# One SBUF pool moves behind three others: u's high and low parts go from 16K to 104K of a partition

## The chip, the cores and the metric

The kernel runs on one core of a Trainium2 chip. The metric is device time in microseconds: 467.73 us, the median of three runs (467.04 to 467.74).

## What is computed

One residual block of a decoder with 512 tokens and 1024 channels, all in float32. `u = rms_norm(x)` is multiplied by one wide input matrix (5912 columns). Its columns become the queries, keys, values and gates of two attention branches of 8 heads each (A: compressed, selected and sliding-window attention; B: block-sparse attention), the SiLU gates z of both, and two merge gates:

```python
u = rms_norm(x, norm_pre)
proj = u @ w_in
y_a = nsa_attention(...) * silu(z_a);  y_b = moba_attention(...) * silu(z_b)
m = sigmoid(gate_a) * (y_a @ w_a) + sigmoid(gate_b) * (y_b @ w_b)
out = x + rms_norm(m @ w_o, norm_post)
```

At 512 tokens all blocks that could be selected are selected, so the attention of both branches is causal over whole 512-token rows.

## The kernel before

**Two parts for each operand.** Every float32 operand of a large product is split into a high part and a low part (the rest), and a product is three matmuls: high by high, high by low, low by high. `u` lies transposed in two tiles `uh` and `ul`, 128 partitions by 8 slices of 512 tokens (16 KB of a partition each). In `mm(out, held, streamed)` the second argument is the operand held in the array, which a weight load (PEld in the profile) brings in before each matmul; the third is streamed through it.

**The work.** The input columns come in chunks of 256: 20 chunks (kcvc, ksw, qa0, qa1, za0, za1, zb0, zb1, qkb0 to 3, ga0 to 3, gb0 to 3) go through `proj`, two halves of 24 matmuls each, which hold a 128x128 piece of the split weights (`ws`, pool `wspl`) and stream 512 tokens of `uh` or `ul` (L171 to L173). That makes 20 x 48 = 960 matmuls that stream u. The two chunks vb0 and vb1 do it the other way round: they hold a piece of `uh` or `ul` and stream 256 columns of `ws` (L294 to L296), 192 matmuls. Four chunks ab0 to ab3 use the same `proj` for `y @ w_a` and `y @ w_b`: they hold `ws` and stream `ys`, y's two parts (192 matmuls of 512 columns). wo0 holds `m`, the merged result, and streams `ws` (L416 to L418, 96 matmuls); wo1 holds `m` and streams `wo1h` (L1118 to L1120).

```python
171            mm(dst, v[:, 0, k], rh(n), start=(n == 0), stop=False)        # rh: uh or ys
172            mm(dst, v[:, 0, k], rl(n), start=False, stop=False)           # rl: ul or ys
173            mm(dst, v[:, 1, k], rh(n), start=False, stop=(n == len(kts) - 1))
294            mm(o, uh[:, kk, a], v[:, 0, k], start=first, stop=False, skip_group_check=True)
416            mm(o, mst[kk][:, 0, a], v[:, 0, k], start=(kk == 0), stop=False)
417            mm(o, mst[kk][:, 0, a], v[:, 1, k], start=False, stop=False)
418            mm(o, mst[kk][:, 1, a], v[:, 0, k], start=False, stop=(kk == KT - 1))
1118           mm(o, mst[k][:, 0, a], wo1h[:, 0, k, w], start=(k == 0), stop=False)
1119           mm(o, mst[k][:, 0, a], wo1h[:, 1, k, w], start=False, stop=False)
1120           mm(o, mst[k][:, 1, a], wo1h[:, 0, k, w], start=False, stop=(k == KT - 1))
```

**The order.** TensorE's order is written out by hand. First the norm and transposes of x and a small projection (to 25.6 us), then kcvc and ksw in one row (96 matmuls), w1 and qa, then the attention of 24 units, 80 to 327 us. Each unit has scores (L953 streams the high part of k, L954 its low part `klos`, both hold q), transposes of the probabilities p (L992), and the product with v (L1008, L1009 stream the transposed p, `pt`, and hold v); between these stand pieces of the projection chunks, most of them three steps of `proj`, so 9 matmuls in a row. Along the timeline the 960 matmuls that stream u stand in 3 rows of 96 (kcvc with ksw, ga2 with gb2, ga3 with gb3), 2 of 24, 5 of 18, 52 of 9, 9 of 6 and 4 of 3. After the attention come ab0, ab1, ga2, gb2, ab2, ga3, gb3, ab3, wo0 and wo1 with the last norm.

**Where the tiles lie.** A pool takes the next free bytes of each partition when it is opened, and each small tile is rounded up to 32 bytes. The first pool begins at byte 16,512 (16K and 128 bytes). The pools in their order, with the byte addresses that follow:

| pool | what it holds | from byte (K) | offset in 512 bytes of its tiles |
|---|---|---|---|
| const, 52,192 bytes | uh, ul, ident, klos, vcs, small ones | 16,512 (16.1K); ul 32,896 | uh, ul 128; klos 160; vcs 96 |
| wraw, 2 x 8 KB | raw weights | 68,704 (67.1K) | 96 |
| wspl, 3 x 8 KB | `ws`, split weights | 85,088 (83.1K) | 96 |
| s4, 12 x 4 KB | shared homes: q, k, v, ys, kcsl, gates, m_4, m_5 | 109,664 (107.1K) | 96 |
| zp, 4 x 4 KB | z, later m_0 to m_3 | 158,816 (155.1K) | 96 |
| small | statistics | 175,200 (171.1K) | |
| early, att, mp in turn | x; pt, p, bias; wo1h, m_6, m_7 | 179,744 (175.5K) | pt, wo1h, m_6, m_7: 32 |

All slices that a matmul takes of these tiles begin at multiples of 512 bytes from there, so the last column holds for them too (a slice of q, k, v, u, ws, ys, m or wo1h).

Of the kernel before, what the change touches and what calls it, by code (L numbers as in the profile page):

```python
# [41 lines left out]
def hybrid_block(ctx, tc, x, norm_pre, w_in, pe_k, w1_k, w2_k, pe_v, w1_v, w2_v,  # L42
# [10 lines left out]
    def enter(**kw):  # L53
        return ctx.enter_context(tc.tile_pool(**kw))

    const = enter(name="const", bufs=1)
    wraw = enter(name="wraw", bufs=2)
    wspl = enter(name="wspl", bufs=3)
    psum = enter(name="psum", bufs=2, space=PSUM)
    s4 = enter(name="s4", bufs=12)  # L60
    zp = enter(name="zp", bufs=4)
    small = enter(name="small", bufs=2)

# [1101 lines left out]
```

## Time and profile before

| | |
|---|---|
| median of 3 runs | 467.73 us |
| profiled execution | 467.33 us, its span 465.6 us |
| granted TensorE clock, mean | 0.997 |
| TensorE busy | 457.3 us (98%) of 2408 matmuls |
| VectorE, ScalarE, GpSimd busy | 322.8, 253.6, 123.4 us |
| moved from and to HBM | 41.6 MB, 89 GB/s over the span |

TensorE's matmuls overlap: one takes some 390 ns from its start to its modelled end, and the next starts before that. What a matmul costs in a full row is therefore read as the distance between two starts, and best over a row of many: (last start - first start) / number of steps. The start times of the timeline have 10 ns, so a row of 20 steps gives 0.5 ns.

### The profile page before, as it was taken

How to read it: one execution, taken by the hardware profiler on the slowest of the kernel's cores; microseconds unless marked ns; L12 is line 12 of the kernel's file. 1: busy time of each engine (PE TensorE's matmuls, PEld its weight loads, DVE VectorE, ACT ScalarE, POOL GpSimd, SP SyncE). 2: the span in 40 equal slices, each digit the busy share in tenths (PEclk: the TensorE clock that was granted, in tenths of full speed). 3: DMA queues.
4: the chain of work that ended last, by engine and by line, in shares of the span. 5: the costliest groups of instructions: out<-in, count | busy, mean ns of one | idle time of the engine just before them, and what ended most of it. 6: DMA issues, size and time to landing. Idle time of an engine off the chain costs nothing.

```text
span 465.6 us, 7014 instructions
## 1 busy us (share of the span) xinstructions
PE 457.3 (98%) x2408; PEld 389.7 (84%) x2408; DVE 322.8 (69%) x830; ACT 253.6 (54%) x684; POOL 123.4 (26%) x143
## 2 busy tenths in 40 slices
PE   8999999999999999999999999999999999999994
PEld 6988887889999888888888888888888888888884
DVE  3868768898878768778897878786674263275044
ACT  5845556666666566566766756675433333234021
POOL 2540008312432313423154454332221020020000
PEclk9999999999999999999999999999999999999998
DMA  8666225023302204032131221132235323223133
GB/s 275 196 181 182 62 49 162 13 80 92 78 15 92 74 18 109 8 88 92 23 114 48 66 92 49 44 92 90 61 103 145 100 52 129 90 90 137 45 137 135
DMA packets 45731, 43.13 MB, mean 93 GB/s; under 512 B 1752, under 2 KB 39936, under 8 KB 45696
## 3 DMA queue, kind: packets, MB, share of 16 engines
q1 hardware_dynamic: 45552, 42.17, 30.9%
q10 hardware_dynamic: 144, 0.52, 0.4%
q8 instruction: 19, 0.31, 0.3%
q14 instruction: 16, 0.13, 0.1%
HBM read 39.54 MB, written 2.10 MB: 89 GB/s over the span
## 4 chain that ended last, share of the span: by engine, by line
PE 97%; DMA 1%; DVE 0%; ACT 0%; SPq 0%; POOLq 0%; issue 0%; POOL 0%; DVEq 0%; ACTq 0%
PE t L992 6%; PE o L1009 3%; PE o L1008 3%; PE s L953 3%; PE mm_ga L171 3%; PE mm_ga L172 3%; PE mm_gb L171 3%; PE mm_gb L172 3%; PE mm_gb L173 3%; PE mm_ga L173 3%; PE mm_qkb L171 3%; PE mm_qkb L172 3%; PE mm_qkb L173 3%; PE s L954 3%; PE pa L640 3%; PE mm_qa L171 2%
## 5 line engine op out<-in xcount | busy, mean ns | idle before, releaser
L959 ACT ACTIVATE p<-p,st 128x512 f32<-128x512 f32 (+3 forms) x96 | 53.2, 555 | 42.0 <-DVE st L957 41.8
L971 POOL TENSOR_SCALAR p<-p,st 128x256 f32<-128x256 f32 (+1 forms) x48 | 43.8, 922 | 68.3 <-DVE st L968 51.5
L994 DVE TENSOR_TENSOR pt<-t,pt 128x512 fp32r<-128x512 f32 (+1 forms) x72 | 39.1, 591 | 3.6 <-ACT pt L993 3.4
L993 ACT ACTIVATE pt<-t 128x512 fp32r<-128x512 f32 (+1 forms) x72 | 32.8, 528 | 9.5 <-PE t L992 9.0
L957 DVE CUSTOM_DVE_ANT_0 p<-s,bias_a 128x512 f32<-128x512 f32 (+3 forms) x64 | 29.1, 485 | 11.4 <-PE s L954 11.1
L358 POOL TENSOR_TENSOR ga<-ga,gb 128x512 f32<-128x512 f32 x8 | 11.7, 1464 | 76.3 <-DVE gb L357 76.3
L992 PE MATMUL t<-ident,p 128*128 128x128 f32 x240 | 30.1, 273 | 0.0
L992 PEld LDWEIGHTS t<-ident,p 128*128 128x128 f32 x240 | 27.1, 141 | 0.8
L1020 POOL TENSOR_TENSOR z<-ot,z 64x512 f32<-64x512 f32 x16 | 20.7, 1293 | 24.3 <-DVE ot L1019 24.3
L119 DVE TENSOR_TENSOR ws_ab<-raw_ab,ws_ab 128x256 fp32r<-128x256 f32 x32 | 12.7, 454 | 20.0 <-ACT ws_ab L118 20.0
L971 DVE TENSOR_SCALAR p<-p,st 128x512 f32<-128x512 f32 (+1 forms) x48 | 25.6, 570 | 0.6
L171 PE MATMUL mm_qkb<-uh,ws_qkb 128*128 128x512 f32 x64 | 25.8, 404 | 0.0
L171 PE MATMUL mm_ga<-uh,ws_ga 128*128 128x512 f32 x64 | 25.6, 400 | 0.0
L171 PE MATMUL mm_gb<-uh,ws_gb 128*128 128x512 f32 x64 | 25.6, 400 | 0.0
L173 PE MATMUL mm_gb<-uh,ws_gb 128*128 128x512 f32 x64 | 25.3, 395 | 0.0
L173 PE MATMUL mm_ga<-uh,ws_ga 128*128 128x512 f32 x64 | 25.3, 395 | 0.0
L172 PE MATMUL mm_ga<-ul,ws_ga 128*128 128x512 f32 x64 | 25.3, 395 | 0.0
L172 PE MATMUL mm_gb<-ul,ws_gb 128*128 128x512 f32 x64 | 25.2, 394 | 0.0
L173 PE MATMUL mm_qkb<-uh,ws_qkb 128*128 128x512 f32 x64 | 25.2, 394 | 0.0
L172 PE MATMUL mm_qkb<-ul,ws_qkb 128*128 128x512 f32 x64 | 25.2, 394 | 0.0
L911 POOL TENSOR_SCALAR bias_b<-dbase 128x512 f32<-128x512 f32 x8 | 12.3, 1535 | 36.7 <-DVE st L957 36.7
L911 POOL TENSOR_SCALAR bias_a<-dbase 128x512 f32<-128x512 f32 x8 | 13.0, 1620 | 33.2 <-DVE st L957 33.0
(309 smaller groups left out, 1379.5 us busy)
## 6 DMA issues: line engine op xcount, KB each, us to landing
raw_qkb<-in_w_in_dram SPq DMA_DIRECT2D x8, 512.0 KB, 5.2
raw_ga<-in_w_in_dram SPq DMA_DIRECT2D x4, 1024.0 KB, 5.5
raw_gb<-in_w_in_dram SPq DMA_DIRECT2D x4, 1024.0 KB, 5.2
raw_wo<-in_w_o_dram SPq DMA_DIRECT2D x4, 1024.0 KB, 5.0
raw_qa<-in_w_in_dram SPq DMA_DIRECT2D x4, 512.0 KB, 6.6
raw_za<-in_w_in_dram SPq DMA_DIRECT2D x4, 512.0 KB, 5.2
raw_vb<-in_w_in_dram SPq DMA_DIRECT2D x2, 1024.0 KB, 5.2
raw_zb<-in_w_in_dram SPq DMA_DIRECT2D x2, 1024.0 KB, 5.7
```

Of the source, the lines that this page charges most:

```text
L171: mm(dst, v[:, 0, k], rh(n), start=(n == 0), stop=False)
L172: mm(dst, v[:, 0, k], rl(n), start=False, stop=False)
L173: mm(dst, v[:, 1, k], rh(n), start=False, stop=(n == len(kts) - 1))
L640: mm(pt[:, 0:280], u[:, k, a], wa_hl[:, h, k], start=(n == 0 and k == 0), stop=(n == last and k == KT - 1))
L911: pool.tensor_scalar(t, dbase, slope, None, op0=ALU.mult)
L957: dve.tensor_tensor_reduce(pp, src, bias[:, 384 - 128 * i:512], 1.0, 3.0e38, ALU.add, ALU.min, st[:, 0, i:i + 1])
L959: act.activation(pp, pp, AF.Exp, bias=st[:, 0, i:i + 1], scale=-1.0, accum_out=st[:, 1, i:i + 1])
L971: (dve if i >= 2 else pool).tensor_scalar(pp, pp, st[:, 1, i:i + 1], None, op0=ALU.mult)
L992: pe_eng.transpose(tp[:, b * 128:(b + 1) * 128], p_of(u, i)[:, 128 * j:128 * j + 128], ident)
L993: act.activation(h[:, c0:c0 + n], tp[:, 0:n], AF.Copy)
L994: dve.tensor_tensor(l[:, c0:c0 + n], tp[:, 0:n], f(h[:, c0:c0 + n]), op=ALU.subtract)
L1020: pool.tensor_tensor(zs[zt][mine], t[mine], zs[zt][mine], op=ALU.mult)
```

## The change

`const` is opened after `s4` instead of first. Nothing else differs.

```diff
-    const = enter(name="const", bufs=1)
     wraw = enter(name="wraw", bufs=2)
     wspl = enter(name="wspl", bufs=3)
     psum = enter(name="psum", bufs=2, space=PSUM)
     s4 = enter(name="s4", bufs=12)
+    const = enter(name="const", bufs=1)
     zp = enter(name="zp", bufs=4)
     small = enter(name="small", bufs=2)
```

By the sizes of the table wraw, wspl and s4 move down by 52,192 bytes (wraw to 16.1K, wspl to 32.1K, s4 to 56.1K), and const moves up by 90,112 bytes (uh to 104.1K, ul to 120.1K, klos to 136.6K). From zp on all stays. psum is another memory.

## Rows read from the trace of the kernel before

**Rows 1.** The page's first part, TensorE: busy time, share of the span, instructions.
```profile
PE 457.3 (98%) x2408; PEld 389.7 (84%) x2408; DVE 322.8 (69%) x830; ACT 253.6 (54%) x684; POOL 123.4 (26%) x143
```

**Rows 2.** The waits of TensorE over the whole span: all that it waited for, us in total, times, longest.
```profile
PE warmup L664 <- DVE warmup L83: 1.4, 1, 1.4
PE ut L592 <- DVE diag L579: 0.7, 1, 0.7
```

**Rows 3.** TensorE's instructions grouped by line and shape: busy us, mean ns of one from its start to its modelled end, idle before. Second part of the product, in a gate chunk (streams ul) and in the two halves of the ab chunks (stream ys).
```profile
L172 PE MATMUL mm_ga<-ul,ws_ga 128*128 128x512 f32 x64 | 25.3, 395 | 0.0
...
L172 PE MATMUL pa<-ys_a,ws_ab 128*128 128x512 f32 x32 | 12.4, 389 | 0.0
...
L172 PE MATMUL pb<-ys_b,ws_ab 128*128 128x512 f32 x32 | 12.4, 389 | 0.0
```

**Rows 4.** Timeline of TensorE in gb3 (streams u): start us, us, engine, line, tiles. The first and the last row shown are 20 steps apart.
```profile
399.33 0.40 PE L171 MATMUL mm_gb<-uh,ws_gb 128*128 128x512 f32 x1
...
404.00 0.40 PE L173 MATMUL mm_gb<-uh,ws_gb 128*128 128x512 f32 x1
```

**Rows 5.** The same timeline, going on: the first eight matmuls of ab3 (streams ys), and two later ones that are 24 steps apart.
```profile
404.23 0.40 PE L171 MATMUL pa<-ys_a,ws_ab 128*128 128x512 f32 x1
404.48 0.39 PE L172 MATMUL pa<-ys_a,ws_ab 128*128 128x512 f32 x1
404.70 0.39 PE L173 MATMUL pa<-ys_a,ws_ab 128*128 128x512 f32 x1
404.93 0.40 PE L171 MATMUL pa<-ys_a,ws_ab 128*128 128x512 f32 x1
405.17 0.39 PE L172 MATMUL pa<-ys_a,ws_ab 128*128 128x512 f32 x1
405.39 0.40 PE L173 MATMUL pa<-ys_a,ws_ab 128*128 128x512 f32 x1
405.63 0.39 PE L171 MATMUL pa<-ys_a,ws_ab 128*128 128x512 f32 x1
405.86 0.39 PE L172 MATMUL pa<-ys_a,ws_ab 128*128 128x512 f32 x1
...
407.22 0.39 PE L172 MATMUL pb<-ys_b,ws_ab 128*128 128x512 f32 x1
...
412.66 0.39 PE L172 MATMUL pb<-ys_b,ws_ab 128*128 128x512 f32 x1
```

**Rows 6.** Timeline of wo0 (holds m, streams ws): its first matmul, and 72 steps later the first one that holds m_6. The 24 steps from there, with m_6 and m_7, end at the first row of group 7.
```profile
415.15 0.39 PE L416 MATMUL wo<-ws_wo,m 128*128 128x512 f32 x1
...
431.47 0.39 PE L416 MATMUL wo<-ws_wo,m 128*128 128x512 f32 x1
```

**Rows 7.** Timeline of wo1 (holds m, streams wo1h): the first matmul, with m_0; 18 steps later the first of the six that hold m_6 and m_7; and the one after these six, with m_0 again.
```profile
436.96 0.39 PE L1118 MATMUL wo<-wo1h,m 128*128 128x512 f32 x1
...
441.16 0.40 PE L1118 MATMUL wo<-wo1h,m 128*128 128x512 f32 x1
441.40 0.39 PE L1119 MATMUL wo<-wo1h,m 128*128 128x512 f32 x1
441.62 0.39 PE L1120 MATMUL wo<-wo1h,m 128*128 128x512 f32 x1
441.86 0.40 PE L1118 MATMUL wo<-wo1h,m 128*128 128x512 f32 x1
442.09 0.39 PE L1119 MATMUL wo<-wo1h,m 128*128 128x512 f32 x1
442.32 0.39 PE L1120 MATMUL wo<-wo1h,m 128*128 128x512 f32 x1
442.55 0.40 PE L1118 MATMUL wo<-wo1h,m 128*128 128x512 f32 x1
```

**Rows 8.** Busy time in three stretches: us, then busy us and instructions of PE, PEld, DVE, ACT, POOL, then granted TensorE clock, DMA share, GB/s. The first streams u, the second is wo1, the third wo0.
```profile
364.00:366.00 2.00, 2.00 (x10) 1.60 (x9) 0.00 (x0) 0.49 (x1) 0.00 (x0) 1.00 0.00 0
...
439.00:441.00 2.00, 2.00 (x10) 1.58 (x10) 0.00 (x0) 0.00 (x0) 0.00 (x0) 1.00 0.00 0
...
415.00:417.00 2.00, 2.00 (x11) 1.65 (x10) 1.65 (x3) 1.15 (x2) 0.88 (x1) 1.00 1.05 408
```

**Rows 9.** Timeline of one row of 9 that stream u, in the attention: the second matmul, and the first score 8 steps later. There are 52 such rows.
```profile
97.66 0.39 PE L172 MATMUL mm_za<-ul,ws_za 128*128 128x512 f32 x1
...
99.52 0.39 PE L953 MATMUL s<-k_ks,q_a 128*128 128x512 f32 x1
```

**Rows 10.** Timeline of matmuls of 256 columns: vb0, two rows 11 steps apart; then wo1's second cut, two rows 5 steps apart with m_4 and m_5 held, and two rows 5 steps apart with m_6 and m_7 held.
```profile
129.01 0.28 PE L294 MATMUL mm_vb<-ws_vb,uh 128*128 128x256 f32 x1
...
130.31 0.28 PE L296 MATMUL mm_vb<-ws_vb,ul 128*128 128x256 f32 x1
...
455.10 0.28 PE L1118 MATMUL wo<-wo1h,m 128*128 128x256 f32 x1
...
455.67 0.28 PE L1120 MATMUL wo<-wo1h,m 128*128 128x256 f32 x1
455.78 0.28 PE L1118 MATMUL wo<-wo1h,m 128*128 128x256 f32 x1
...
456.38 0.28 PE L1120 MATMUL wo<-wo1h,m 128*128 128x256 f32 x1
```

## The prediction

> **What bounds the kernel.** I read the page's first part and TensorE's waits first: TensorE is busy 98% of the span [rows 1], and it waited 2.1 us in all, both times within the start-up [rows 2]. After that no other engine and no DMA holds it up; the time is the sum of the distances between the starts of its matmuls. The change moves only addresses: it adds, removes and reorders no instruction, DMA or wait. So it can act only if a matmul's own pace depends on where its operands lie. I went to the groups by shape to see whether it does, and it does: the same 128x512 matmul on the same line has a mean of 395 ns when it streams ul and 389 ns when it streams ys [rows 3]. The timeline says what that is per step. In gb3, 20 steps take 404.00 - 399.33 = 4.67 us, 233.5 ns each [rows 4]. In ab3, once it runs evenly, 24 steps take 412.66 - 407.22 = 5.44 us, 226.7 ns each [rows 5]; wo0's first 72 take 431.47 - 415.15 = 16.32 us, again 226.7 [rows 6]; wo1's first 18 take 441.16 - 436.96 = 4.20 us, 233.3 [rows 7]. There are two paces, 233.3 and 226.7 ns, 6.6 ns apart.
>
> The clock is not the reason: it is granted in full, the 2.4 GHz level, in stretches of all three kinds. Nor is other traffic: wo1 goes at 233.3 in a stretch where VectorE, ScalarE, GpSimd and DMA do nothing at all, u's stretch is nearly as quiet, and wo0 goes at 226.7 with the DMA engines at a share of 1.05 and three engines busy [rows 8]. The addresses are left. Two accounts fit the even stretches.
>
> *Offset.* What counts is the distance between the streamed operand and the held one, whose next piece is loaded while the present one streams, within 512 bytes (the last column of the table of pools). ab streams 96 and holds 96: distance 0, 226.7. wo0 with m_0 to m_5: 96 and 96, 0, 226.7. u's matmuls: 128 - 96 = 32, 233.5. wo1 with m_0 to m_5: 32 - 96 = -64, 233.3. wo0 with m_6 and m_7: 96 - 32 = 64, and its 24 steps take 436.96 - 431.47 = 5.49 us, 228.8 ns [rows 6, 7].
>
> *Place.* Every pair at 226.7 lies with both operands between 83K and 172K of the partition; u (16K to 48K) and wo1h (179K to 212K) lie outside.
>
> One stretch separates them. In wo1 the six steps with m_6 and m_7 have distance 0 (32 and 32), but both operands lie above 179K. They should be slow by place. By offset they should do what ab3 does when it comes in from another distance, and it takes ab3 seven steps to run evenly: the lengths are 0.40, 0.39, 0.39, 0.40, 0.39, 0.40 [rows 5]. The six steps of wo1 show 0.40, 0.39, 0.39, 0.40, 0.39, 0.39, and their starts stand alike, the first step long (0.25 and 0.24 us), the second short (0.22 in both), then 0.22 to 0.24; that is 1.39 us / 6 = 231.7 ns on average, under the 233.3 before them [rows 5, 7]. They enter the even pace as ab3 does; six steps are too few to reach it. That is why I take the offset account.
>
> **The change part by part, by offset.** const moves up by 90,112 bytes, 176 x 512, so uh, ul, klos and vcs keep their offsets. wraw, wspl and s4 move down by 52,192 bytes, 101 x 512 + 480, so their offset goes from 96 to 128. zp and what lies behind it stay.
>
> 1. *u streams, ws held: 32 becomes 0.* 960 matmuls. In a row of 96 the first steps are the entry. ab3's entry of seven steps takes 405.86 - 404.23 = 1.63 us, 232.9 ns each [rows 5], so the entry gains nothing over 233.3, and each step after it gains 6.6 ns. In the rows of 9 the pace now is (99.52 - 97.66) / 8 = 232.5 ns [rows 9], so a step there gains 5.8. How long the entry is after a score, a transpose or a product with v, no row shows for distance 0. Seven steps is the long end, from ab3; the short end is one. I take four, as the entries here do not come out of the 233.3 pattern that ab3 came from. Rows of 96: 3 x 91 x 6.6 = 1.80 us. Rows of 24: 2 x 19 x 6.6 = 0.25. Of 18: 5 x 13 x 5.8 = 0.38. Of 9: 52 x 4 x 5.8 = 1.21. Of 6: 9 x 1 x 5.8 = 0.05. Sum -3.7 us; with entries of seven steps -2.5, with one step -5.0.
> 2. *vb: ws streams, u held, -32 becomes 0.* 192 matmuls of 256 columns. Now (130.31 - 129.01) / 11 = 118.2 ns. At distance 0 the only row of this shape is wo1 with m_6 and m_7: (456.38 - 455.78) / 5 = 120 ns; the fastest that this shape shows anywhere is (455.67 - 455.10) / 5 = 114 ns [rows 10]. I take 120, the row with the same distance: 192 x 1.8 = +0.35 us; the other end is 192 x -4.2 = -0.8.
> 3. *wo0 with m_0 to m_3 (zp): 0 becomes 32.* 48 matmuls go from 226.7 to 233.3: +0.32 us. With m_4 and m_5 both operands move alike: 0. With m_6 and m_7 64 becomes 96, which no row shows: between 226.7 and 233.3 from 228.8 now, -0.05 to +0.1 us.
> 4. *ab, and the high part of k against q:* both operands lie in wspl or s4 and move alike: 0.
> 5. *The rest of the attention.* klos against q goes from 64 to 32, pt against v from -64 to -96, wo1 with m_4 and m_5 likewise, w1's two chunks shift too. These are some 300 matmuls, and no row shows -96. With the two paces as ends each could gain or lose up to 3 ns on average: -0.9 to +0.9 us. I take 0.
> 6. *The other engines* run the same instructions on tiles that lie elsewhere. TensorE waits for none of them [rows 2], so it costs nothing, as long as they keep their lead; with TensorE 0.7% faster and VectorE at 69% [rows 1] I put nothing on a wait that comes out.
>
> Sum: -3.7 + 0.35 + 0.32 = -3.0 us. The profiled execution took 467.33 us (span 465.6), 0.4 under the median of the runs, so the sum gives 464.3 for it and 464.7 for a median; I say 464.5. The ends: -5.0 - 0.8 + 0.3 - 0.9 = -6.4, and -2.5 + 0.35 + 0.4 + 0.9 = -0.9; all terms will not fall on one side, so this case's own range is 462.0 to 466.4.
>
> **A rule against it.** The rows show two steady paces for one form of instruction with the clock at full [rows 4, 5, 8]. The Trainium skill, "TensorE: Matmul & The Clock Gate", in its Part 2 ("Step-by-step"), says that the array reads the streamed and the held operand through two independent ports, so that loading the next weights takes nothing from the running matmul; under "Back-to-back issue gap" it gives 215.7 ns for 512 columns as its figure. By that, addresses play no part and the change is worth 0: 467.3 to 467.7. The trace does not agree with it, at 226.7 and 233.3.
>
> **Rivals.**
> - *Place of both operands (slower).* The even pace needs both operands between 83K and 172K, and one outside costs the full 6.6 ns. u is then inside, but ws, at 32K to 56K, is out: u's matmuls stay at 233.3. ab holds ws and loses 192 x 6.6 = 1.27 us, wo0 streams it and loses 72 x 6.6 = 0.48 with m_0 to m_5 and 24 x 4.5 = 0.11 with m_6 and m_7. That is +1.9 us, 469.4. It decides if a held operand alone at 32K is enough to slow a stream from 104K. For it: all even stretches lie inside. Against it: the six steps of wo1 [rows 7], and m_6 held at 211K cost wo0 2.1 ns a step, not 6.6 [rows 6]. Chance 0.09.
> - *Place of the streamed operand alone (faster still).* u goes to 226.7 at once, entries and all: 960 x 6.3 = -6.0 us; wo0 streams ws from below and loses 0.6, and half of ab's ys, now at 56K to 83K, 96 x 6.6 = 0.6. That is -4.8, 462.7. Against it is the same stretch of wo1. Chance 0.10.
> - *Nothing.* The pace hangs on neither, but on the kind of row (which lines alternate, which PSUM bank), and the time stays at 467.3 to 467.9. Against it: gb3 and ab3 go through the same lines with the same shape [rows 4, 5]. The rule of independent ports in the Trainium skill's page above would end here too. Chance 0.13.
> - *Offset, but short rows eat it.* Entries longer than nine steps, and the unknown distances of part 5 at their bad end: -1.8 - 0.25 + 0.35 + 0.32 + 0.9 = -0.5 us. Chance 0.04.
>
> **Numbers.** The offset account has 0.64. What a measurement of this kernel can tell is about 0.2%, 0.9 us. Faster by more than that: 0.64 + 0.10 = 0.74. Within it: 0.13 + 0.04 = 0.17. Slower: 0.09. The predicted time is the offset account's, 464.5. The range goes down to 461.8 for the streamed operand's place, and up to 467.7, which takes in about half of the cases without a difference.
>
> **What would show it.** Right: gb3's 20 steps at 226.7 ns after the first few, the mean of the L172 matmuls in ga near 389, rows of 9 with 2 to 6 even steps, wo0's first 48 steps at 233.3 and the next 24 at 226.7, vb at 120. Place of both: gb3 at 233.3 and ab3 no longer at 226.7. Streamed operand's place: the rows of 9 even from the second step on, wo0 slow throughout. I am wrong in the main step if gb3's pace stays, and wrong in the size if the entries are longer or shorter than four steps or if klos and pt change their pace.

## The result, and the profile after

| | before | after |
|---|---|---|
| median | 467.44 us (467.04 to 467.74, 4 runs) | 464.36 us (464.17 to 464.89, 4 runs) |
| profiled execution, its span | 467.33 us, 465.6 us | 464.53 us, 462.7 us |

The ratio of the times is 0.9936, with an interval of 0.9924 to 0.9948: 0.6% faster. Each engine runs the same instructions in the same order. The page's first part and TensorE's waits, which answer to [rows 1, 2]:

```profile
PE 454.5 (98%) x2408; PEld 390.6 (84%) x2408; DVE 322.8 (70%) x830; ACT 253.9 (55%) x684; POOL 123.8 (27%) x143
```

```profile
PE warmup L664 <- DVE warmup L83: 1.4, 1, 1.4
PE ut L592 <- DVE diag L579: 0.8, 1, 0.8
```

TensorE still waits for nothing after the start-up, and its busy time fell by 457.3 - 454.5 = 2.8 us; the span lost 465.6 - 462.7 = 2.9. So the difference is in the pace of the matmuls. The groups by shape (busy us, mean ns of one, idle before); the first two answer to [rows 3], the last one is wo0:

```profile
L172 PE MATMUL mm_ga<-ul,ws_ga 128*128 128x512 f32 x64 | 25.0, 390 | 0.0
...
L172 PE MATMUL pa<-ys_a,ws_ab 128*128 128x512 f32 x32 | 12.4, 389 | 0.0
...
L417 PE MATMUL wo<-ws_wo,m 128*128 128x512 f32 x32 | 12.6, 394 | 0.0
```

The gate chunk, which streams u, went from 395 to 390 ns; ab stayed; wo0 became slower. Its line before was:

```profile
L417 PE MATMUL wo<-ws_wo,m 128*128 128x512 f32 x32 | 12.5, 390 | 0.0
```

The timeline gives the steps. The end of gb3 and the start of ab3 [rows 4, 5]:

```profile
396.51 0.39 PE L172 MATMUL mm_gb<-ul,ws_gb 128*128 128x512 f32 x1
...
401.05 0.39 PE L171 MATMUL pa<-ys_a,ws_ab 128*128 128x512 f32 x1
401.27 0.39 PE L172 MATMUL pa<-ys_a,ws_ab 128*128 128x512 f32 x1
401.50 0.39 PE L173 MATMUL pa<-ys_a,ws_ab 128*128 128x512 f32 x1
```

In gb3, 20 steps now take 401.05 - 396.51 = 4.54 us, 227.0 ns each, where they took 233.5. And ab3 has no entry any more: its first steps are as short as gb3's, since the distance between streamed and held operand is 0 in both. wo0 [rows 6] went the other way:

```profile
411.94 0.39 PE L416 MATMUL wo<-ws_wo,m 128*128 128x512 f32 x1
...
423.13 0.39 PE L416 MATMUL wo<-ws_wo,m 128*128 128x512 f32 x1
...
428.58 0.39 PE L416 MATMUL wo<-ws_wo,m 128*128 128x512 f32 x1
...
434.17 0.39 PE L1118 MATMUL wo<-wo1h,m 128*128 128x512 f32 x1
```

These are 48 steps with m_0 to m_3, 24 with m_4 and m_5, and 24 with m_6 and m_7: 11.19 / 48 = 233.1 ns, 5.45 / 24 = 227.1, 5.59 / 24 = 232.9. The row of 9 that answers to [rows 9], and vb [rows 10]:

```profile
96.92 0.39 PE L172 MATMUL mm_za<-ul,ws_za 128*128 128x512 f32 x1
97.15 0.40 PE L173 MATMUL mm_za<-uh,ws_za 128*128 128x512 f32 x1
97.39 0.39 PE L171 MATMUL mm_za<-uh,ws_za 128*128 128x512 f32 x1
97.62 0.40 PE L172 MATMUL mm_za<-ul,ws_za 128*128 128x512 f32 x1
...
98.31 0.39 PE L172 MATMUL mm_za<-ul,ws_za 128*128 128x512 f32 x1
98.53 0.39 PE L173 MATMUL mm_za<-uh,ws_za 128*128 128x512 f32 x1
98.76 0.39 PE L953 MATMUL s<-k_ks,q_a 128*128 128x512 f32 x1
```

```profile
128.31 0.28 PE L294 MATMUL mm_vb<-ws_vb,uh 128*128 128x256 f32 x1
...
129.63 0.28 PE L296 MATMUL mm_vb<-ws_vb,ul 128*128 128x256 f32 x1
```

The row of 9 takes 1.84 / 8 = 230.0 ns a step (232.5 before). In the trace's nanoseconds its steps are 231, 235, 229, 232, 231, 227, 226, 227: five uneven ones, the entry, and then three even ones. vb's 11 steps take 1.32 / 11 = 120.0 ns.

The whole difference, as sums of the distances from each matmul's start to the next one's, over all rows of the two traces (us):

| group | matmuls | before | after | difference |
|---|---|---|---|---|
| u streams, ws held | 960 | 226.31 | 222.24 | -4.08 |
| vb | 192 | 23.07 | 23.27 | +0.21 |
| wo0 | 96 | 21.81 | 22.24 | +0.42 |
| klos; k's high part | 88; 88 | 14.59; 14.92 | 14.78; 14.88 | +0.19; -0.04 |
| pt with v | 192 | 30.65 | 30.82 | +0.17 |
| ab; wo1 | 192; 119 | 43.61; 22.26 | 43.58; 22.24 | -0.03; -0.01 |
| the start-up and the rest | 480 | 60.57 | 60.93 | +0.37 |
| all | 2407 | 457.79 | 454.98 | -2.81 |

### The profile page after: what moved, and what is told of

Read it like the earlier page. It is cut to its first block, busy times and chain, and to the rows that moved or that the text cites. A ratio compares the mean times of both kernels' runs of the same rounds, so it can differ in the third digit from the quotient of the medians.

```text
span 462.7 us, 7014 instructions
## 1 busy us (share of the span) xinstructions
PE 454.5 (98%) x2408; PEld 390.6 (84%) x2408; DVE 322.8 (70%) x830; ACT 253.9 (55%) x684; POOL 123.8 (27%) x143
## 4 chain that ended last, share of the span: by engine, by line
PE 97%; DMA 1%; DVE 0%; ACT 0%; SPq 0%; POOLq 0%; POOL 0%; issue 0%; DVEq 0%; ACTq 0%
PE t L992 6%; PE o L1009 3%; PE o L1008 3%; PE s L953 3%; PE s L954 3%; PE mm_qkb L173 3%; PE mm_qkb L171 3%; PE mm_qkb L172 3%; PE mm_ga L171 3%; PE mm_ga L173 3%; PE mm_gb L173 3%; PE mm_gb L171 3%; PE mm_ga L172 3%; PE mm_gb L172 3%; PE pa L640 3%; PE mm_qa L171 2%
```

## The experiments

The theory was the distance between streamed and held operand; its rivals were the place in the partition, and that the pace hangs on neither. The first five kernels change addresses, as the change does, and beside them only add one or two memsets of the unused bytes on GpSimd. The last two run rows of matmuls without the rest of the block; each of these ran once, with a granted clock of 1.00.

**The distance without the move.** `x1_pad32` keeps the order of the pools of before, so u stays at 16K, and puts 32 unused bytes at the end of const. All that lies behind it shifts by 32 bytes: ws, ys and m from offset 96 to 128, pt, wo1h and m_6 from 32 to 64.

```diff
     vcs = const.tile([128, 2, 2, 128], F32R, name="vcs")
+    pad = const.tile([128, 8], F32, name="pad")
+    pool.memset(pad, 0.0)
```

> The order of the pools as before, u at 16K; only 32 unused bytes are put behind the last tile of const, so that wraw, wspl, s4 and all behind them lie 32 bytes higher. Streamed u against held ws: distance 32 becomes 0. Distances among the pools behind const do not change, so wo0, wo1, ab and pt against v keep theirs. Offset: u's steps go to 226.7 ns after the entries, as in the changed kernel, where they are 4.1 us less in sum; wo0 stays at 226.7, so 0.3 us better than the changed kernel: 463.8 to 464.4 us. Place (of both operands, or of the streamed one): nothing moved by more than 32 bytes, so 467.4 us, as before. Nothing: 467.4.

Measured: 463.86 us (463.75 to 463.94, 5 runs) beside 467.37 of before, ratio 0.9923 (0.991 to 0.9937). Two of its groups, and gb3's timeline:

```profile
L172 PE MATMUL mm_ga<-ul,ws_ga 128*128 128x512 f32 x64 | 25.0, 390 | 0.0
...
L417 PE MATMUL wo<-ws_wo,m 128*128 128x512 f32 x32 | 12.5, 390 | 0.0
```

```profile
395.24 0.39 PE L171 MATMUL mm_gb<-uh,ws_gb 128*128 128x512 f32 x1
...
399.77 0.39 PE L173 MATMUL mm_gb<-uh,ws_gb 128*128 128x512 f32 x1
```

gb3's 20 steps take 4.53 us, 226.5 ns, with u where it was before. The 960 matmuls lost 4.04 us against 4.08 in the change. wo0 keeps its pace (21.81 us), because m and ws shift together. So 32 unused bytes bring what the move brought; by the median it is 0.5 us more, of which wo0 is 0.42, but the intervals of the two ratios overlap.

**The move without the distance.** `x2_dist32` has the changed order of pools, u at 104K, and lets uh and ul, and ident behind them, begin 32 bytes later, so that u's distance is 32 again. (Two small tiles become one, so that const keeps its length.)

```diff
-    const = enter(name="const", bufs=1)
...
     s4 = enter(name="s4", bufs=12)
+    const = enter(name="const", bufs=1)
...
+    pad = const.tile([128, 8], F32, name="pad")
+    pool.memset(pad, 0.0)
     uh = const.tile([128, KT, T], F32R, name="uh")
...
-    neghalf = const.tile([128, 1], F32, name="neghalf")
...
+    two1 = const.tile([128, 2], F32, name="two1")
+    neghalf, warm = two1[:, 0:1], two1[:, 1:2]
...
-    warm = const.tile([128, 1], F32, name="warm")
```

> The changed order of the pools, u at 104K; only uh and ul lie 32 bytes higher, so that their distance to ws is 32 again, as in the kernel before; klos and all else lie as in the changed kernel (a constant shares a small tile to make room). Offset: u's steps are back at 233.3 ns, wo0 with m_0 to m_3 stays at 233.3 as in the changed kernel, so the gain is gone: 467.4 to 468.2 us. Place of the streamed operand: u still lies inside, 464.4 us, as the changed kernel.

Measured: 468.44 us (468.22 to 469.07, 9 runs), ratio 1.0022 (1.0013 to 1.0032): slower than before. The gate chunk's group, and gb3's timeline:

```profile
L175 PE MATMUL mm_ga<-ul,ws_ga 128*128 128x512 f32 x64 | 25.3, 395 | 0.0
```

```profile
399.04 0.40 PE L174 MATMUL mm_gb<-uh,ws_gb 128*128 128x512 f32 x1
...
403.70 0.40 PE L176 MATMUL mm_gb<-uh,ws_gb 128*128 128x512 f32 x1
```

20 steps take 4.66 us, 233.0 ns, and u's sum is +0.22 us against before. What is left of the change are its losses, above all wo0 +0.42 and pt +0.28. Another +0.28 us are in a small projection of the start-up that holds u (L642 there). That is no slower pace: the last 54 of its 96 steps take 7.05 us against 7.04 before, and ahead of these TensorE waits:

```profile
PE pa L642 <- ACT uh L606: 0.3, 1, 0.3
```

The move alone is worth nothing or less.

**All distances at 0.** `x3_all_zero` takes before's order and brings u, ws, ys, m, klos, vcs, pt and wo1h all to offset 128: neghalf goes behind klos, 32 bytes stand ahead of vcs, and a pool of 64 bytes behind small. `x4_all_zero_104K` is the same with const opened behind s4.

```diff
     small = enter(name="small", bufs=2)
+    pad2 = enter(name="pad2", bufs=1).tile([128, 16], F32, name="pad2")
+    nc.gpsimd.memset(pad2, 0.0)
...
-    neghalf = const.tile([128, 1], F32, name="neghalf")
-    pool.memset(neghalf, -0.5)
...
     klos = [const.tile([128, 2, 2, T], F32R, name=f"klos{i}") for i in range(2)]
...
+    neghalf = const.tile([128, 1], F32, name="neghalf")
+    pool.memset(neghalf, -0.5)
...
+    pad = const.tile([128, 8], F32, name="pad")
+    pool.memset(pad, 0.0)
     vcs = const.tile([128, 2, 2, 128], F32R, name="vcs")
```

> The order of the pools as before, u at 16K, with 32 unused bytes ahead of vcs, 64 behind the pool of statistics, and one small constant behind klos, so that uh, ul, klos, ws, q, k, v, ys, m, pt, vcs, pc and wo1h all begin at offset 128 of 512 bytes: distance 0 for nearly all matmuls. Offset: u's gain as with 32 bytes alone; wo1's 72 matmuls of 512 go from 232.8 to near 226.7 (-0.4 us), wo0 with m_6 and m_7 -0.05, k, klos and pt rows could gain up to 3 ns each on some 300 matmuls (-0.9) or lose some where 256 columns go at 120: 462.6 to 464.2 us. Place: 467.4 us.

> The order of the pools of the changed kernel (u at 104K, ws at 32K, q, k, v, ys at 56K to 104K) with the same small shifts as in the kernel with everything at distance 0. Offset: the same time as that kernel with u at 16K, 462.9 to 463.4 us. Place, as a second effect beside the offset: another time, up to 1.9 us above if one operand outside 83K to 172K costs something, or below if u gains by its place.

Measured: `x3_all_zero` 463.13 us (462.92 to 463.32, 4 runs), ratio 0.9908 (0.9894 to 0.9921); `x4_all_zero_104K` 463.45 us (463.01 to 463.73, 4 runs) beside 467.39, ratio 0.9914 (0.9899 to 0.9929). They agree within what can be told, and no group's sum differs by more than 0.03 us between them but the one with the start-up (0.12), so the place has no effect of its own. Both are below before; the interval of the first lies below that of the change, that of the second overlaps it. In `x3_all_zero` wo1 has the even pace too, though its operands lie where they lay in before but for these few bytes (m_0 to m_5 below 172K, wo1h above 175K). Its first matmul and the one 18 steps on [rows 7]:

```profile
433.21 0.39 PE L1122 MATMUL wo<-wo1h,m 128*128 128x512 f32 x1
...
437.29 0.39 PE L1122 MATMUL wo<-wo1h,m 128*128 128x512 f32 x1
```

That is 4.08 / 18 = 226.7 ns. Against before u has -3.97 us, wo1 -0.30, wo0 -0.05, vb +0.23; klos (+0.03) and pt (+0.11) gained nothing from distance 0.

**The period.** `x5_pad288` is `x1_pad32` with a pad of 288 bytes: a distance of -256 instead of 0.

```diff
+    pad = const.tile([128, 72], F32, name="pad")
+    pool.memset(pad, 0.0)
```

> As the kernel with 32 unused bytes behind const's last tile, but 288 bytes: the distance of u to ws is 32 - 288 = -256. The rows of matmuls alone had the same pace at 256 as at 0, so by the offset with a period of 256 bytes this gives the same time, 463.6 to 464.2 us; with a period of 512 bytes u stays at 233.3 and the time at 467.4 us. Place: 467.4.

Measured: 463.77 us (463.59 to 464.78, 4 runs), ratio 0.9929 (0.9912 to 0.9945), u -4.02 us. All groups but those of the start-up agree with `x1_pad32` within 0.02 us. What counts repeats after 256 bytes already, not after 512 as the prediction had it.

**Distance by itself.** `mb_distance` runs rows of 48 matmuls, one after the other, each with one distance d. w_a to w_p have 512 columns and d = 0, 32, ..., 480; z and y have d = 0 and 32, with the streamed and the held operand low (30K and 16K) or high (158K and 144K), z*hl* being held high, streamed low; n_a to n_p have 256 columns and d = 0, 32, ..., 480.

```diff
+        o = d // 4
+        s = streamed[:, o:o + 8192].rearrange("p (h k c) -> p h k c", h=2, k=8)
...
+        for r in range(reps):
+            for k in range(8):
+                for a, b in ((0, 0), (0, 1), (1, 0)):
+                    mm(pt[:, 0:n], h[:, a, k], s[:, b, k, 0:n], start=(i == 0), stop=(i == total - 1))
```

> Leaves out the whole block; it copies x to the output and measures matmul rows alone, with nothing else running. Rows of 48 matmuls in the order of the product of parts (held high with streamed high and low, held low with streamed high), held pieces of 128 columns, streamed slices of 512 columns. Rows w_a to w_p: held at 16K, streamed from 30K, distance 0, 32, 64 ... 480 bytes. Then held low and streamed at 158K (lh), held at 144K and streamed low (hl), both high (hh), each at distance 0 (z) and 32 (y). Then n_a to n_p: 256 columns streamed at distances 0 to 480. Offset: the last 24 steps of w_a at 226.7 ns, w_b (32) at 233.3, w_o (448, that is -64) at 233.3, w_c (64) between; z rows at 226.7 and y rows at 233.3 at all four places; n_a at 120, n_p (480, -32) at 118. Place: all w rows alike whatever the distance, at 233.3, and the pairs of places differ; z and y alike at each place.

The timeline of TensorE, one line for each row (start us, us; the distance between two starts is 48 steps):

```profile
20.68 11.04 PE L80 MATMUL w_a<-str_low,held_low 128*128 128x512 f32 x48
31.55 11.37 PE L80 MATMUL w_b<-str_low,held_low 128*128 128x512 f32 x48
42.76 11.16 PE L80 MATMUL w_c<-str_low,held_low 128*128 128x512 f32 x48
53.76 11.37 PE L80 MATMUL w_d<-str_low,held_low 128*128 128x512 f32 x48
...
109.79 11.05 PE L80 MATMUL w_i<-str_low,held_low 128*128 128x512 f32 x48
120.67 11.37 PE L80 MATMUL w_j<-str_low,held_low 128*128 128x512 f32 x48
...
198.91 11.05 PE L80 MATMUL zlh<-str_high,held_low 128*128 128x512 f32 x48
209.79 11.37 PE L80 MATMUL ylh<-str_high,held_low 128*128 128x512 f32 x48
221.00 11.08 PE L80 MATMUL zhl<-str_low,held_high 128*128 128x512 f32 x48
231.91 11.37 PE L80 MATMUL yhl<-str_low,held_high 128*128 128x512 f32 x48
243.12 11.08 PE L80 MATMUL zhh<-str_high,held_high 128*128 128x512 f32 x48
254.03 11.37 PE L80 MATMUL yhh<-str_high,held_high 128*128 128x512 f32 x48
265.24 5.93 PE L80 MATMUL n_a<-str_low,held_low 128*128 128x256 f32 x48
271.00 5.82 PE L80 MATMUL n_b<-str_low,held_low 128*128 128x256 f32 x48
276.66 5.82 PE L80 MATMUL n_c<-str_low,held_low 128*128 128x256 f32 x48
```

w_a takes 31.55 - 20.68 = 10.87 us, 226.5 ns a step; w_b 11.21 us, 233.5; w_c 11.00, 229.2; w_d 11.21. From w_i on (256 bytes) it is the same series again. By the last 24 steps of each row: 226.67 at 0, 233.33 at 32, 228.88 at 64, 233.3 to 234.2 at all others up to 224. The z rows take 10.88 to 10.91 us and the y rows 11.21, at each of the places. zhl and zhh, which follow on a row with distance 32, need seven steps to run even, and their starts stand as ab3's did [rows 5]; w_i and zlh, which follow on 224, are even after one step. With 256 columns distance 0 is not the fast one: 120.0 ns against 117.8 at 32 and 64.

**Finer steps.** `mb2_fine` uses the same rows for distances that are no multiples of 32, for both operands shifted together, for a held piece that never changes, for pieces whose offsets alternate between 0 and 32, and for 384 columns.

```diff
-        h = held[:, 0:2048].rearrange("p (h k c) -> p h k c", h=2, k=8)
-        o = d // 4
+        h = held[:, e // 4:2048 + e // 4].rearrange("p (h k c) -> p h k c", h=2, k=8)
+        o = (d + e) // 4
```

> Leaves out the whole block; it copies x to the output and measures rows of 48 matmuls as the first measurement of distances did. f rows: distances 4, 8, 12, 16, 20, 24, 28 bytes; b rows: 252, 240, 228. e rows: distance 0, with both operands 4, 16, 32, 64, 96 bytes higher; g rows: distance 32, both 16, 32, 64, 96 higher. altown: pieces of 128 columns are held that lie alternately at 0 and 32 of 512, and each streamed slice lies at the offset of its own held piece (so at distance 32 from the next one); altnext: each streamed slice lies at the offset of the next held piece (distance 32 from its own). same rows: one held piece all the time, distances 0, 32, 96. m rows: 256 columns at distances 4, 8, 16, 24; t rows: 384 columns at 0, 32, 96, 160. Offset with the next load as the partner, as predicted: altnext at 226.7 ns, altown at 233.3; e rows all 226.7, g rows all 233.3; same as the w rows of that distance. Its rival, that the piece in the array counts: altown at 226.7, altnext at 233.3. If the matter is whole 32- or 64-byte lines, distances 4 to 28 go at one of the paces of 0 and 32; if it is finer, they go between or even under 226.7.

```profile
20.48 11.04 PE L80 MATMUL zfirst<-str_low,held_low 128*128 128x512 f32 x48
31.36 11.59 PE L80 MATMUL f_a<-str_low,held_low 128*128 128x512 f32 x48
42.78 11.36 PE L80 MATMUL f_b<-str_low,held_low 128*128 128x512 f32 x48
...
143.59 11.57 PE L80 MATMUL e_a<-str_low,held_low 128*128 128x512 f32 x48
155.00 11.25 PE L80 MATMUL e_b<-str_low,held_low 128*128 128x512 f32 x48
166.09 11.05 PE L80 MATMUL e_c<-str_low,held_low 128*128 128x512 f32 x48
176.97 11.08 PE L80 MATMUL e_d<-str_low,held_low 128*128 128x512 f32 x48
...
288.29 11.09 PE L96 MATMUL same_a<-str_low,held_low 128*128 128x512 f32 x48
299.21 11.37 PE L96 MATMUL same_b<-str_low,held_low 128*128 128x512 f32 x48
```

The edit is against `mb_distance`: e bytes are added to both operands. zfirst has distance 0, f_a 4, f_b 8; e_a to e_d have distance 0 and both operands shifted by 4, 16, 32 and 64 bytes; same_a and same_b hold one piece at distance 0 and 32. Distance 4 costs 42.78 - 31.36 = 11.42 us, 237.9 ns a step. Both operands shifted by 4 at distance 0 (e_a) cost 11.41, as much; shifted by 16 (e_b) 11.09, 231.0; shifted by 32 (e_c) 10.88, nothing. So 32 bytes may be added to both, as may 64 and 96 (226.67 ns over the last 24 steps), but not 4 or 16. The row that holds one piece all the time behaves like the others (same_a 10.92 us, same_b 11.21). With alternating pieces neither form ran even, 233.9 ns where the streamed operand matched its own piece and 231.7 where it matched the next. The first lies near the 233.3 that was expected if the partner is the piece loaded meanwhile, and far from the 226.7 if it is the piece in the array; the second fits neither. So the partner stays open. With 384 columns it is 173.3 ns at 0, 32 and 160, and 176.7 at 96.

## Why the prediction was right

The step that carries it, two paces that hang on the distance between the operands, held. 464.5 was said, 464.36 came.

1. **u:** the term was -3.7 us and measured -4.08. By kind of row: 96 steps -1.89 (said -1.80), 24 -0.24 (-0.25), 18 -0.38 (-0.38), 9 -1.50 (-1.21), 6 -0.07 (-0.05). I had taken an entry of four steps and no gain in it. In the rows of 9 the entry is longer: 5.2 of the eight steps between their matmuls on average, three in most rows behind a score, seven or more in most behind a transpose, and 16 of the 52 rows never run even. That leaves 148 even steps where 208 were taken. They gave 6.8 ns each instead of 5.8, which is -1.00 us; the steps of the entry, said to gain nothing, gave 1.3 ns each, -0.34; and the step from the row's last matmul to the next group, which I had left out, gave -0.17. In the rows of 96 two of three have no entry at all.
2. **vb:** 120.0 ns came as taken from the six steps of wo1 [rows 10]; the sum is +0.21 instead of +0.35, because 120.0 against 118.2 holds for the even stretches alone. Over all 192 steps, with the first steps of the rows, the averages are 23.07 / 192 = 120.2 ns before and 23.27 / 192 = 121.2 after.
3. **wo0:** +0.42, as the sum of +0.32 and the upper bound +0.1: m_6 and m_7 at distance 96 went to 232.9 ns.
4. **ab and k:** -0.03 and -0.04, said 0.
5. **The rest of the attention:** klos +0.19 and pt +0.17, said 0 within 0.9. For klos the reason lies near: 64 became 32, and the even rows of `mb_distance` have 228.9 and 233.3 ns there. pt's is not settled: in `x1_pad32`, where its distance to v did not change, it lost 0.40 us. What runs around it may count too: in the changed kernel and `x2_dist32` p, pt and v lie alike, only u and ident lie elsewhere, and pt's sum differs by 0.11 us.
6. **Other engines:** TensorE's waits are the same two.

The rest, +0.37 us, is in the group that holds the start-up: kcvc's first matmul starts at 26.17 us instead of 25.84. Of it +0.22 us are in the first matmuls of the program (`warmup`), of which one more steps at some 427 ns before they run at 227, and +0.10 in the transposes of x, whose wait went from 0.7 to 0.8 us. Among the experiments the group goes from -0.33 (`x5_pad288`) to +0.39 us (`x2_dist32`) against before; `x1_pad32`, whose distances equal those of `x5_pad288` modulo 256, is at -0.17. What moves it no run shows, and the prediction had no term for it.

That the sum came so near is in part luck: u gave 0.38 us more than said, and klos, pt and the start-up together took 0.73 that had been put at 0. The terms for u, vb and wo0, -3.45 us as measured, are what the mechanism answers for.

The rivals: place of both operands falls with gb3 (held at 32K, streamed at 104K, even pace) and with `mb_distance`; place of the streamed operand falls with `x1_pad32` and `x2_dist32`, which part place and distance; no effect at all falls with the ratio's interval, and short rows that eat the gain fall with the rows of 9, which gave 1.50 us. Where the prediction's account was too wide is the period: it spoke of 512 bytes, and 256 is enough. No distance of the change told the two apart, so the number did not suffer.

By the rule that I weighed, two independent ports (the Trainium skill, "TensorE: Matmul & The Clock Gate", Part 2, "Step-by-step"), the rows of `mb_distance` should all have one pace. They have 226.7, 228.9 and 233.3 ns, so for this form of matmul the measurement decides against what I drew from it, that addresses play no part. The 215.7 ns that the prediction puts under "Back-to-back issue gap" stand under "Step-by-step" of that page; no even row of 512 columns here comes below 226.5. Whether the two operands share a port, and why the distance matters inside the engine, no run here shows.

## What to carry to other kernels

In a kernel that TensorE bounds, compare the steps of even rows of one shape: where two rows of the same shape differ by a few per cent with no wait and the clock in full, look at the byte offsets of the two operands within 256 bytes. Here it was settled with 96 unused bytes and one small tile put elsewhere, for 0.9%, without moving a pool. It paid in rows of 512 columns of some length: klos, whose matmuls alternate with k's, gained nothing from distance 0, and vb, with 256 columns, lost 0.2 us. What a large move in memory seems to bring can be such a remainder, and it should be tried with the remainder alone.

## What the runs showed of the hardware

- A 128x512 matmul of this kind (fp32r, weights loaded each time) steps at 226.67 ns at distance 0 modulo 256, 228.88 at 64, 233.3 to 234.2 at the other multiples of 32, and from 228.6 (28 bytes) to 240.0 (20 bytes) at the distances tried that are no multiple of 32.
- The place in the partition, 16K or 144K held, 30K or 158K streamed, changed none of it at the distances 0 and 32.
- A row whose distance is 0 may run unevenly for some steps first, and how many hangs on what ran before: seven after distance 32, one after 224, three in most rows behind a score, seven or more in most behind a transpose.
- With 256 columns the order turns: 117.8 ns at 32 and 64, 120.0 at 0, and 116.7 at 16. With 384 columns 0 and 32 are alike, 173.3 ns.
